# Last head's stores on GpSimd's queue, the last pair's inputs loaded before the final loop, the last convolution group kept in SBUF, and sums interleaved with splits

## The chip, the cores and the metric

The kernel runs on one core of a Trainium2 chip. The core has five engines with a queue each: TensorE (PE in the profile; PEld is its weight load), VectorE (DVE), ScalarE (ACT), GpSimd (POOL) and SyncE (SP). SyncE, ScalarE and GpSimd can start DMA transfers; the rows that end in q (SPq, ACTq) are such issues. An engine runs its queue in order, and waits at an instruction whose inputs or whose buffer aren't ready. The metric is the time of one execution on the device in microseconds (us).

## What is computed

One layer over 1024 latent tokens of width 1024, with 256 context tokens. Cut to what matters:

```python
shift, scale, gate = adaln(c, w_ada, b_ada)
h  = rmsnorm(x, norm_g) * (1 + scale) + shift
hc = rmsnorm(ctx, norm_g) * (1 + scale_c) + shift_c
q, k, v, za, u, bg, cg, zc = split(h @ w_in)       # eight groups of 512 columns
q, k = rmsnorm(heads(q), q_norm_g), rmsnorm(heads(k), k_norm_g)
kc, vc = split(hc @ w_in[:, 512:1536])              # kc is normed too
attn = neighbourhood_attention(q, k, v, kc, vc, rpb) * silu(za)    # 8 heads of 64
conv = bg * conv3(cg * u, conv_w, conv_b) * silu(zc)
out = x + gate * (concatenate([attn, conv]) @ w_out)
```

Everything is in 32-bit floats. Attention sees a clamped window of 8 by 16 tokens of the 16 by 64 grid and all context tokens in one softmax.

## The kernel before

**Tiles.** A tile has 128 partitions. Activations are held transposed: features on partitions, 1024 tokens along the row. The features of the concatenated branches are eight blocks f of 128: 0 to 3 are the four pairs of attention heads, 4 to 7 the four convolution groups. A 32-bit product is made of three matmuls: each operand is split into a high part (a cast on ScalarE) and a low part (a subtraction on VectorE), and high by high, high by low and low by high are summed in PSUM. `split` makes such a pair; `split_right` does it for activations and `split_left` for weights.

**Stages.** First the modulation and the norm, then the projection of q, k and v, then the attention of eight heads, and last the output projection. The gates and convolutions are not a stage of their own: they are cut into ticks of six matmuls, and `fill` (a generator over `attn_group` and `conv_group`) issues a tick at chosen points of the attention (`TICKS`). A `unit` is one column block of 128 outputs of w_in: two halves of 512 tokens, four ticks each, 48 matmuls, and each half has a PSUM bank of the tag "U", of which there are two. `chore` queues the ScalarE and VectorE work that follows; `do_acts` and `do_dves` issue it.

**The attention's end.** The last convolution group is `conv_group(3)`. When the attention's last quarter is issued, two ticks of its gate (the SiLU's argument) and its whole last unit (48 matmuls) are left. In `conv_group`, `gates` multiplies the convolution by the SiLU and `gains` by the last unit; `times` does either, and at the second it stores the half to `y_d` in DRAM. `head.finish` copies a head's sums and its output out of PSUM and stores them to `rs_d` and `o_d`; the queue is SyncE's, for the last head ScalarE's. The last pair of heads is then gated in pieces: `recip` loads the sums, takes reciprocals on VectorE and stores them to `ri_d`; `load_sums` loads them spread over partitions (`rb`); `z_d` holds the gate's argument, which is loaded into `zs` and goes through SiLU; and o_d, zs and rb are multiplied. The loop over the rest of `fill` at line 1432 issues one tick, then the queued chores, then `step(k)`, which holds a piece of the output projection's preparation.

**The output projection.** It is one step of a fast matrix multiplication: the 1024 by 1024 by 1024 product is cut into two by two by two blocks of 512 and made of seven products (numbered 1 to 7) instead of eight. `K_HALVES` says which feature blocks form the two halves of the inner dimension: 4, 5, 6, 0 and 1, 2, 3, 7. `combined(q)` makes the sums and differences of activation blocks, on VectorE; those of the weights lie in `w_d` from before. `load_left` loads the four raw weight blocks of a product into one of two buffers "A" and "B". `product(q, ps)` runs 48 matmuls: four inner blocks, four output tiles, three matmuls. The products run in the order 1, 5, 2, 6, 3, 7, 4. `four("SSCC")` takes the banks of the accumulator `a`, into which products 1, 6, 7 and 4 are summed in turn; `four("OOUU")` takes four others, which products 5, 2 and 3 use one after another. `residual` loads a tile of x (named m), `add` adds a bank times the gate to it (VectorE), and `put` stores it.

**What sets the order.** In the projection and the attention, instructions of TensorE, ScalarE, VectorE and GpSimd run in the order in which the program issues them (`ordered`, `strict`); from line 1340 SyncE's transfers do too. The split buffers have six ("left") and eight ("right") places in each of two pools, `op` and `rp`; a place is written again when TensorE has read it. `rp` lies where the activations of the input projection were. All instructions carry line 71 in the profile, since they are recorded by the wrapper there; the transfers of the attention carry their own lines.

Of the kernel before, what the change touches and what calls it, by code (L numbers as in the profile page):

```python
# [10 lines left out]
F32 = mybir.dt.float32  # L11
F32R = mybir.dt.float32r
BF16 = mybir.dt.bfloat16
AF = mybir.ActivationFunctionType
ALU = mybir.AluOpType
# [4 lines left out]
P = 128  # L20
D = 1024
T = 1024
# [4 lines left out]
NH, HD = 8, 64  # L27
# [28 lines left out]
def body(tc, es, x, xb, xt, cb_, ct, w_mod, w_gate, b_ada, w_grp, w_col, q_g, k_g, bias, w_out, vecs, cst, out):  # L56
# [309 lines left out]
        chore(on_act, on_dve)  # L366

    loaded = {}
    ahead = {}
    follows = {}  # L370

# [27 lines left out]
    def blocked(v):  # L399
        return v.rearrange("p (b r c) -> p b r c", b=2, r=16)  # L400

    def by_row(v):
        return v.rearrange("p (r b c) -> p b r c", r=16, b=2)
# [7 lines left out]
    def conv_group(i, done=None):  # L411
# [52 lines left out]
                taps(*work.pop(0))  # L464

        def times(half, v, last):
            dve.tensor_tensor(by_row(cvs[half][:]), blocked(v), by_row(cvs[half][:]), ALU.mult)
            if last:
                sp.dma_start(y_d[4 + i][:, half * 512:(half + 1) * 512], cvs[half])

        def gains():
# [389 lines left out]
    class head:  # L861
# [91 lines left out]
        def finish(self):  # L953

            sums = ap.tile([P, 256], F32, name="sums", tag="sums", bufs=1)
            act.copy(sums[:].rearrange("p (r c) -> p r c", c=16), self.tot[:, :256].rearrange("p (c r) -> p r c", r=16))
            queue = sp if self.h + 1 < NH else act
            queue.dma_start(rs_d[self.p][self.s].rearrange("b (x c) -> (b x) c", c=256),
                          sums[:].rearrange("(x o) c -> x o c", o=32)[:, 0])
            ob = ap.tile([P, 512], F32, name="ob", tag="ob", bufs=1)  # L960
            act.copy(blocked(ob[:]), self.po.rearrange("p (b c r) -> p b r c", b=2, r=16))
            for bank in range(2):
                queue.dma_start(o_d[self.p][64 * self.s:64 * self.s + 64, bank * 512:(bank + 1) * 512], ob[64 * bank:64 * bank + 64])  # L963
# [281 lines left out]
    vts = [prp.tile([P, NB + 2, HD], F32, name=f"v{i}", tag=f"v{i}") for i in range(2)]  # L1245
    ri_last = prp.tile([P, 64], F32, name="ri")

    left_raw, raw_y = {}, {}

    def left_rows(q, i):  # L1250

        if q in (1, 2, 4):
# [8 lines left out]
        for i in range(4):  # L1261
            sp.dma_start(left_raw[q][:, i], left_rows(q, i))

    def load_y(v, f, queue=None):
        (queue or sp).dma_start(v, y_d[f])
        raw_y[f] = v.rearrange("p (a n) -> p a n", a=2)

    def early_loads(n):
# [116 lines left out]
    def split_left(q, pl, steps=range(4)):  # L1385
        for i in steps:
            left[q, i] = split(pl, "left", 6, left_raw[q][:, i], lambda v: v)
# [27 lines left out]

    def step(k):

        if k == 2:
            for _ in reciprocals:
                pass  # L1420
        if k < 4:
            split_right(1, op, [k])
            split_left(1, op, [k])
        if k in (4, 5):
            combined(5, range(2 * k - 8, 2 * k - 6))
        if k in (5, 6):
            split_right(5, op, range(2 * k - 10, 2 * k - 8))
        if k in (7, 8):
            split_left(5, op, [k - 7])

    late = [op.tile([P, T], F32, name="y", tag="y", bufs=2)[:] for _ in range(2)]
    for k, _ in enumerate(fill):
        do_dves()
        do_acts()
        step(k)
    while soon or slow:
        do_dves()
        do_acts()
    hs.close()
    rp = es.enter_context(sbuf("rp", side="right"))  # L1440

    last = NPAIR - 1
    raw_y[last] = late[0].rearrange("p (a n) -> p a n", a=2)
    parts = []
    for half in range(2):
        cols = slice(half * 512, (half + 1) * 512)
        zs, rb = (rp.tile([P, 512], F32, name=n, tag="t", bufs=4) for n in ("zs", "rb"))
        sp.dma_start(zs, z_d[last][:, cols])
        sp.dma_start(raw_y[last][:, half], o_d[last][:, cols])
        load_sums(last, half, rb, pool)  # L1450
        parts.append((raw_y[last][:, half], zs, rb))
    load_y(late[1], 7, pool)
    load_left(2, "A")
    m12, m22 = zip(*[(residual(c, 1), residual(4 + c, 1)) for c in every_tile])
    m11 = [residual(c, 0) for c in every_tile]

    split_right(2, rp, range(2))
    split_left(5, op, [2])
    for tb, zs, rb in parts:
        act.activation(zs, zs, AF.Silu)  # L1460
        dve.tensor_tensor(tb, tb, zs, ALU.mult)
        dve.tensor_tensor(tb, tb, rb, ALU.mult)
    split_left(5, op, [3])
    load_left(6, "B")
    split_left(2, rp)
    split_right(2, rp, range(2, 4))
    combined(6)
    split_right(6, rp)

    a = four("SSCC")  # L1470
    c5 = four("OOUU")
# [1 line left out]
    for c in every_tile:  # L1473
        product(5, c5, [c], first=True)
        add(c5[c], c, m12[c])
        add(c5[c], 4 + c, m22[c])
    for c in every_tile:
        add(a[c], c, m11[c])
    load_left(3, "A")
    c2_ = four("OOUU")  # L1480
    product(2, c2_, first=True)
    split_left(6, rp)
# [1 line left out]
    split_right(3, op)  # L1484
    split_left(3, op)
    load_left(4, "A")
    combined(7)
    split_right(7, op)
    combined(4)
    for c in every_tile:  # L1490
        add(c2_[c], c, m11[c])
        put(m11[c], c, 0)
    for c in every_tile:
        product(6, a, [c])
    m21 = [residual(4 + c, 0) for c in every_tile]
# [12 lines left out]
    for c in every_tile:  # L1508
        product(7, a, [c])
        add(a[c], 4 + c, m22[c])  # L1510
        put(m22[c], 4 + c, 1)
    head_, tail = slice(0, 384), slice(384, 512)
    for c in range(3):
        product(4, a, [c])
        add(a[c], 4 + c, m21[c])
        put(m21[c], 4 + c, 0)
    end = {3: bank("pout", "O")}
    add(a[3], 7, m21[3], tail)
    product(4, a, [3], cols=head_)
    product(4, end, [3], first=True, cols=tail)  # L1520
    add(a[3], 7, m21[3], head_)
# [64 lines left out]
```

## Time and profile before

| What | Value |
| --- | --- |
| Median of 3 runs | 603.13 us (602.87 to 603.36) |
| The profiled execution | 603.09 us |
| Its span, first to last instruction | 601.3 us |
| TensorE busy | 585.5 us |
| VectorE busy | 439.8 us |
| ScalarE busy | 285.8 us |
| GpSimd busy | 56.7 us |
| Mean granted TensorE clock | 0.997 of full speed |
| Moved by DMA | 127.16 MB |

The profiled execution takes 1.8 us more than its span, for what lies ahead of the first and behind the last instruction. In a timeline row stand the start, the time taken, the engine, the operation with its tiles (out<-in, partitions by elements), how many alike are merged into the row, and in brackets the idle time before it with what ended that. In a row of merged instructions the time goes from the start of the first to the end of the last. In a row of windows stand, for each engine, the busy time and the number of instructions, then the granted clock of TensorE, the mean busy share of the 16 DMA engines and GB/s.

### The profile page before, as it was taken

Reading aid. Unit: us, or ns where it says so; the run is one execution under the profiler, and the core shown is the slowest. Engines: PE = TensorE matmul, PEld = TensorE weight load, DVE = VectorE, ACT = ScalarE, POOL = GpSimd, SP = SyncE. Lnnn points to the kernel's source line nnn. Section 1 sums busy time; section 2 is a strip of 40 time slices with the busy share of each in tenths; the row PEclk is TensorE's granted clock in tenths of the full one; section 3 lists DMA queues with packets and bytes.
Section 4 is the critical chain, followed back from the end, with each engine's and each line's share of the span. In section 5 each row is a group of like instructions: output and inputs, shape, how many; then the busy total and the mean of one; then the engine's idle time right before and its main releaser. Section 6 shows DMA issues by size and latency. Waiting matters only on the chain. (4 is left out here: it accounts for less than half of the span.)

```text
span 601.3 us, 9494 instructions
## 1 busy us (share of the span) xinstructions
PE 585.5 (97%) x3307; PEld 493.0 (82%) x3308; DVE 439.8 (73%) x898; ACT 285.8 (48%) x660; POOL 56.7 (9%) x80
## 2 busy tenths in 40 slices
PE   8999999999999999999999999999999998989997
PEld 3567899999999999888878787878878776867886
DVE  1576879756837745458989797999798896589952
ACT  6645355436526445434554473646456446345220
POOL 1001024123223232100000000000000001100000
PEclk9999999999999999999999999999999998999999
DMA  8996476945756694766162829274955631693532
GB/s 311 416 417 228 179 246 189 312 157 201 262 182 224 230 334 172 280 237 221 53 236 101 289 80 309 85 273 134 327 165 190 197 120 33 198 377 109 183 118 87
DMA packets 67148, 127.16 MB, mean 211 GB/s; under 512 B 8737, under 2 KB 27673, under 8 KB 64796
## 3 DMA queue, kind: packets, MB, share of 16 engines
q1 hardware_dynamic: 66532, 125.22, 59.8%
q0 software_dynamic: 400, 1.07, 0.5%
q8 instruction: 26, 0.43, 0.3%
q10 hardware_dynamic: 168, 0.27, 0.2%
q14 instruction: 22, 0.18, 0.1%
HBM read 92.90 MB, written 33.62 MB: 210 GB/s over the span
## 5 line engine op out<-in xcount | busy, mean ns | idle before, releaser
L71 PE MATMUL pu<-h,uh 128*128 128x512 f32 x544 | 173.3, 400 | 2.9 <-ACT zs L71 2.9
L71 PE MATMUL pacc<-w,h 128*128 128x384 f32 x768 | 138.9, 337 | 0.9 <-ACT ub L71 0.5
L71 PEld LDWEIGHTS pacc<-w,h 128*128 128x128 f32 x768 | 132.7, 188 | 1.8 <-ACT ub L71 0.9
L71 PEld LDWEIGHTS pu<-h,uh 128*128 128x128 f32 x544 | 98.1, 190 | 22.0 <-ACT zs L71 3.3
L71 PE MATMUL pu<-h,ul 128*128 128x512 f32 x272 | 107.3, 394 | 0.0
L71 PE MATMUL pout<-right,left 128*128 128x512 f32 (+2 forms) x348 | 78.6, 385 | 4.4 <-DVE m L71 3.3
L71 PEld LDWEIGHTS pout<-right,left 128*128 128x128 f32 x348 | 63.9, 188 | 19.2 <-DVE m L71 3.8
L71 PEld LDWEIGHTS pu<-h,ul 128*128 128x128 f32 x272 | 51.4, 189 | 11.6
L71 POOL TENSOR_TENSOR ss<-ss,few 128x4 f32<-128x4 f32 (+1 forms) x40 | 41.4, 1036 | 126.7 <-DVE ss L71 126.4
L71 ACT ACTIVATE sc<-sc 128x512 f32<-128x512 f32 x32 | 20.2, 633 | 37.9 <-DVE sc L71 37.9
L71 PE MATMUL acc<-h,w 128*128 128x512 f32 x144 | 37.2, 403 | 0.8 <-ACT h L71 0.8
L71 ACT ACTIVATE sq<-pacc 128x256 f32<-128x256 f32 x32 | 12.4, 387 | 46.4 <-PE pacc L71 45.7
L71 ACT COPY mg<-pmx 128x256 f32<-128x256 f32 (+1 forms) x33 | 12.1, 367 | 47.0 <-issue 22.8
L71 PEld LDWEIGHTS acc<-h,w 128*128 128x128 f32 x144 | 25.8, 188 | 9.0 <-ACT h L71 1.7
L71 DVE TENSOR_TENSOR sum<-sum,sb 128x372 f32<-128x372 f32 (+2 forms) x64 | 31.0, 485 | 2.7
L71 ACT ACTIVATE qn<-pacc,ss 128x64 f32<-128x64 f32 x128 | 30.1, 331 | 4.9 <-PE trA L71 2.5
L71 DVE TENSOR_TENSOR mx<-mx,sb 128x372 f32<-128x372 f32 (+2 forms) x64 | 30.9, 483 | 1.9
L71 DVE SCALAR_TENSOR_TENSOR m<-pout,ab,m 128x512 f32<-128x512 f32 (+2 forms) x34 | 22.5, 715 | 13.3 <-PE pout L71 13.3
L71 DVE TENSOR_REDUCE ss<-sq 128x4 f32<-128x260 f32 (+1 forms) x40 | 15.7, 392 | 21.1 <-ACT sq L71 21.1
L71 DVE TENSOR_TENSOR ul<-uraw,uh 128x512 fp32r<-128x512 f32 x34 | 23.1, 685 | 10.0 <-ACT uh L71 10.0
L71 DVE TENSOR_TENSOR sb<-pss,bt 128x192 f32<-128x192 f32 (+3 forms) x48 | 27.5, 601 | 2.8 <-PE pss L71 2.8
L71 ACT CAST left<-wraw 128x512 fp32r<-128x512 f32 x28 | 16.3, 618 | 26.9 <-PE pout L71 11.5
(142 smaller groups left out, 893.7 us busy)
## 6 DMA issues: line engine op xcount, KB each, us to landing
uraw<-in_w_col SPq DMA_DIRECT2D x34, 256.0 KB
slab<-in_w_mod SPq DMA_DIRECT2D x8, 1024.0 KB
q_d<-qs SPq DMA_DIRECT2D x32, 256.0 KB
k_s<-k_d SPq DMA_DIRECT2D x8, 1024.0 KB
q_s<-q_d SPq DMA_DIRECT2D x16, 512.0 KB
wr<-in_w_grp SPq DMA_DIRECT2D x40, 192.0 KB
bt<-in_rpb SPq DMA_DIRECT2D x8, 564.0 KB
xn<-in_xb SPq DMA_DIRECT2D x8, 512.0 KB
```

The costliest lines, as they stand in the source:

```text
L71: i = emit(*a, **kw)
```

## The change

1. `head.finish`: the last head's three stores (sums, and the output in two halves) are issued on GpSimd's queue instead of ScalarE's.
2. `conv_group`, `times`: the last group's last product is written into the tile `raw_y[7]` in SBUF instead of in place; the two stores to `y_d` and the load of `y_d[7]` go.
3. The loop over the rest of `fill`: `step` runs one tick later (k - 1). The last pair's inputs (z_d into `zs`, o_d into `raw_y[last]`) are loaded ahead of the loop, in tiles of their own in `op`; `rb`'s first half is loaded at step 1, right behind the reciprocals; the two SiLUs of `zs` and `load_left(2, "A")` come at step 4. The reciprocals move from step 2 to step 1, so they stay at the same tick.
4. Behind the loop: only `rb`'s second half is loaded; `load_left(6, "B")` goes ahead of the residuals m11; the gating of the last pair is cut into `attended(0)` and `attended(1)`, which stand at other places; the splits of product 2's weights are cut in two; `load_left(3, "A")` moves up.
5. Product 5's loop: `split_right(6)` is issued in pieces behind the sums of tiles 1, 2 and 3 instead of ahead of all products.
6. The sums of product 2 and their stores come ahead of `combined(7)`.
7. The sum of the tail of a[3] comes ahead of the loop over product 4's first three tiles.

```diff
@@ conv_group, times
-            dve.tensor_tensor(by_row(cvs[half][:]), blocked(v), by_row(cvs[half][:]), ALU.mult)
-            if last:
+            here = raw_y[7][:, half] if last and i == 3 else cvs[half][:]
+            dve.tensor_tensor(by_row(here), blocked(v), by_row(cvs[half][:]), ALU.mult)
+            if last and i < 3:
                 sp.dma_start(y_d[4 + i][:, half * 512:(half + 1) * 512], cvs[half])
@@ head.finish
-            queue = sp if self.h + 1 < NH else act
+            queue = sp if self.h + 1 < NH else pool
@@ step and the loop
-        if k == 2:
+        if k == 1:
             for _ in reciprocals:
                 pass
+            load_sums(last, 0, rb[0], pool)
         if k < 4:
             split_right(1, op, [k])
             split_left(1, op, [k])
+        if k == 4:
+            for half in range(2):
+                act.activation(zs[half], zs[half], AF.Silu)
+            load_left(2, "A")
         if k in (4, 5):
             combined(5, range(2 * k - 8, 2 * k - 6))
         if k in (5, 6):
             split_right(5, op, range(2 * k - 10, 2 * k - 8))
-        if k in (7, 8):
-            split_left(5, op, [k - 7])
-
-    late = [op.tile([P, T], F32, name="y", tag="y", bufs=2)[:] for _ in range(2)]
+        if k in (6, 7):
+            split_left(5, op, [k - 6])
+
+    last = NPAIR - 1
+    halves_of = [slice(half * 512, (half + 1) * 512) for half in range(2)]
+    for f in (last, 7):
+        raw_y[f] = op.tile([P, T], F32, name="y", tag="y", bufs=2)[:].rearrange("p (a n) -> p a n", a=2)
+    zs = [op.tile([P, 512], F32, name="zs", tag="zs", bufs=2) for _ in halves_of]
+    rb = [op.tile([P, 512], F32, name="rb", tag="rb", bufs=1)]
+    for half, cols in enumerate(halves_of):
+        sp.dma_start(zs[half], z_d[last][:, cols])
+    for half, cols in enumerate(halves_of):
+        sp.dma_start(raw_y[last][:, half], o_d[last][:, cols])
     for k, _ in enumerate(fill):
         do_dves()
         do_acts()
-        step(k)
+        if k:
+            step(k - 1)
...
-    last = NPAIR - 1
-    raw_y[last] = late[0].rearrange("p (a n) -> p a n", a=2)
-    parts = []
-    for half in range(2):
-        cols = slice(half * 512, (half + 1) * 512)
-        zs, rb = (rp.tile([P, 512], F32, name=n, tag="t", bufs=4) for n in ("zs", "rb"))
-        sp.dma_start(zs, z_d[last][:, cols])
-        sp.dma_start(raw_y[last][:, half], o_d[last][:, cols])
-        load_sums(last, half, rb, pool)
-        parts.append((raw_y[last][:, half], zs, rb))
-    load_y(late[1], 7, pool)
-    load_left(2, "A")
+    rb.append(rp.tile([P, 512], F32, name="rb", tag="t", bufs=4))
+    load_sums(last, 1, rb[1], pool)
     m12, m22 = zip(*[(residual(c, 1), residual(4 + c, 1)) for c in every_tile])
+    load_left(6, "B")
     m11 = [residual(c, 0) for c in every_tile]
 
+    def attended(half):
+
+        v = raw_y[last][:, half]
+        dve.tensor_tensor(v, v, zs[half], ALU.mult)
+        dve.tensor_tensor(v, v, rb[half], ALU.mult)
+
+    split_left(5, op, [2])
+    attended(0)
     split_right(2, rp, range(2))
-    split_left(5, op, [2])
-    for tb, zs, rb in parts:
-        act.activation(zs, zs, AF.Silu)
-        dve.tensor_tensor(tb, tb, zs, ALU.mult)
-        dve.tensor_tensor(tb, tb, rb, ALU.mult)
     split_left(5, op, [3])
-    load_left(6, "B")
-    split_left(2, rp)
+    split_left(2, rp, range(2))
     split_right(2, rp, range(2, 4))
+    split_left(2, rp, range(2, 4))
+    load_left(3, "A")
+    attended(1)
     combined(6)
-    split_right(6, rp)
@@ the products
         product(5, c5, [c], first=True)
         add(c5[c], c, m12[c])
         add(c5[c], 4 + c, m22[c])
+        if c:
+            split_right(6, rp, ((), (0, 1), (2,), (3,))[c])
     for c in every_tile:
         add(a[c], c, m11[c])
-    load_left(3, "A")
     c2_ = four("OOUU")
     product(2, c2_, first=True)
...
     load_left(4, "A")
+    for c in every_tile:
+        add(c2_[c], c, m11[c])
+        put(m11[c], c, 0)
     combined(7)
     split_right(7, op)
     combined(4)
-    for c in every_tile:
-        add(c2_[c], c, m11[c])
-        put(m11[c], c, 0)
...
     head_, tail = slice(0, 384), slice(384, 512)
+    add(a[3], 7, m21[3], tail)
     for c in range(3):
         product(4, a, [c])
         add(a[c], 4 + c, m21[c])
         put(m21[c], 4 + c, 0)
     end = {3: bank("pout", "O")}
-    add(a[3], 7, m21[3], tail)
     product(4, a, [3], cols=head_)
```

More of the change, by code (lines that the diff above doesn't have):

```diff
@@ L368, in body @@
     loaded = {}
+    left_raw, raw_y = {}, {}
     ahead = {}
@@ L1246, in body @@
     ri_last = prp.tile([P, 64], F32, name="ri")
-    left_raw, raw_y = {}, {}
     def left_rows(q, i):
@@ L1262, in load_left, with load_y @@
             sp.dma_start(left_raw[q][:, i], left_rows(q, i))
-    def load_y(v, f, queue=None):
-        (queue or sp).dma_start(v, y_d[f])
+    def load_y(v, f):
+        sp.dma_start(v, y_d[f])
         raw_y[f] = v.rearrange("p (a n) -> p a n", a=2)
```

## The prediction

> **What bounds the kernel now.** I read the busy table, then a table of windows over the last fifth, then TensorE's timeline there, and after that the timelines of ScalarE, VectorE, GpSimd and SyncE around each hole.
>
> ```profile
> PE 585.5 (97%) x3307; PEld 493.0 (82%) x3308; DVE 439.8 (73%) x898; ACT 285.8 (48%) x660; POOL 56.7 (9%) x80
> 487.00:490.00 3.00, 2.58 (x12) 2.17 (x13) 2.87 (x7) 1.71 (x3) 0.00 (x0) 1.00 0.50 173
> 499.00:502.50 3.50, 0.58 (x4) 0.16 (x2) 1.29 (x2) 3.12 (x5) 0.77 (x1) 1.00 0.35 77
> 502.50:507.50 5.00, 5.00 (x15) 3.97 (x16) 4.08 (x8) 3.48 (x7) 0.55 (x1) 0.66 0.00 0
> 526.00:538.50 12.50, 11.30 (x49) 8.71 (x47) 10.10 (x17) 6.79 (x12) 0.00 (x0) 1.00 1.04 380
> 538.50:543.50 5.00, 2.91 (x10) 1.51 (x10) 5.00 (x9) 0.20 (x1) 0.00 (x0) 1.00 0.56 211
> 487.43 0.32 PE L71 MATMUL pmx<-ci,rm 128*128 128x128 f32 x1 [0.45 <-DVE rm L71]
> 499.14 0.39 PE L71 MATMUL pu<-h,ul 128*128 128x512 f32 x1
> 502.44 0.73 PE L71 MATMUL pu<-h,uh 128*128 128x512 f32 x2 [2.92 <-ACT zs L71]
> 515.08 13.54 PE L71 MATMUL pout<-right,left 128*128 128x512 f32 x59
> 529.75 8.68 PE L71 MATMUL pout<-right,left 128*128 128x512 f32 x37 [1.13 <-DVE left L71]
> 539.59 0.94 PE L71 MATMUL pout<-right,left 128*128 128x512 f32 x3 [1.16 <-DVE m L71]
> 540.82 0.96 PE L71 MATMUL pout<-right,left 128*128 128x512 f32 x3 [0.29 <-DVE m L71]
> 542.13 0.96 PE L71 MATMUL pout<-right,left 128*128 128x512 f32 x3 [0.35 <-DVE m L71]
> 543.45 49.93 PE L71 MATMUL pout<-right,left 128*128 128x512 f32 x219 [0.36 <-DVE m L71]
> 594.48 3.64 PE L71 MATMUL pout<-right,left 128*128 128x384 f32 x24 [1.10 <-DVE m L71]
> ```
>
> In a window row the columns are each engine's busy time, the granted TensorE clock, the DMA share and GB/s. TensorE is busy for 97% of the span, so almost nothing can be won beside its holes, and all that the change touches starts after 496 us. I measure a hole from start to start, because the end of a last matmul holds its latency too. The pitch of back-to-back matmuls is (49.93 - 0.39) / 218 = 0.2272 us, from the row of 219 (0.39 is the duration of a lone one, at 499.14).
>
> Losses against that pitch: from 499.14 to 502.44 are 3.30 us for one matmul, loss **3.07**. From 502.44 to 515.08 are the 48 matmuls of the last unit, 12.64 against 10.91: loss **1.73**, which is the clock: 5.00 us at 0.66 lose 1.70. From 515.08 to 529.75 are 59 matmuls: 14.67 against 13.40, loss **1.27**. From 529.75 to 539.59 are 37: 9.84 against 8.41, loss **1.43**. Then three groups of 3 matmuls (0.68 each) take 1.23, 1.31 and 1.32: losses **0.55**, **0.63**, **0.64**. From 543.45 to 594.48 are 219: 51.03 against 49.76, loss **1.27**. The sum is 10.6 us. The change can win at most this, beside the tail of about 3 us after the last matmul, which it leaves as it is.
>
> **First hole and slow clock.** The matmul at 502.44 writes the bank of the gate's first half, which the first SiLU frees.
>
> ```profile
> 496.67 0.37 ACT L71 COPY sums<-ptot 128x256 f32<-128x256 f32 x1 [3.09 <-issue]
> 496.94 0.59 ACT L71 COPY ob<-po 128x512 f32<-128x512 f32 x1
> 497.08 1.07 ACTq L958 DMA_DIRECT2D rs_d<-sums  x1
> 497.42 0.63 ACT L71 CAST uh<-uraw 128x512 fp32r<-128x512 f32 x1
> 498.19 1.12 ACTq L963 DMA_DIRECT2D o_d<-ob  x2
> 499.35 0.62 ACT L71 CAST right<-y 128x512 fp32r<-128x512 f32 x1 [1.29 <-issue]
> 499.87 0.61 ACT L71 CAST left<-wraw 128x512 fp32r<-128x512 f32 x1
> 500.50 1.28 ACT L71 ACT_TABLE_LOAD   x1
> 501.80 1.09 ACT L71 ACTIVATE zs<-pu 128x512 f32<-128x512 f32 x2
> ```
>
> ScalarE ends the weight cast at 498.05 and computes nothing until 499.35, while it issues the last head's two output stores: 1.30 us. Then come two casts of step(0), 499.35 to 500.50: 1.15 us. Then the table load of SiLU, then the first SiLU, behind which the matmul starts at 502.44. The change sends the three stores to GpSimd and runs step(0) a tick later, behind the SiLUs. So the table load can follow the cast: 498.05 instead of 500.50, 2.45 earlier. The matmul starts at 499.99, where the pitch wanted 499.37. Of the 3.07 us, 0.62 stay: **2.45 gained**. The second SiLU needs the gate's second half, whose last matmul ends at 499.53, so it isn't held.
>
> The clock falls after the hole of 2.92 us. After holes of 0.45 (at 487.43), 1.13 (at 529.75) and 1.16 (at 539.59) the windows show 1.00. With a hole near half a microsecond I take the drop as gone: **1.70 gained**. Its bounds are 0 and 1.73. The Trainium skill, "TensorE: Matmul & The Clock Gate", Part 1, says that the gate halves the clock after at least one idle window of some 3.4 us; the hole here was shorter, so by that rule the hole alone would not explain the drop, and the loss could stay. The trace has the drop right behind its only long hole, which I follow; the other answer is a rival below.
>
> What the three stores cost on GpSimd is bounded by these rows.
>
> ```profile
> 499.43 0.77 POOL L526 DMA_DIRECT2D ri<-rs_d  x1 [106.62 <-DMA rs_d<-sums]
> 506.39 0.55 POOL L529 DMA_DIRECT2D ri_d<-ri  x1 [6.20 <-DVE ri L71]
> 508.73 1.05 POOL L533 DMA_DIRECT2D rb<-ri_d  x2 [1.78 <-DMA ri_d<-ri]
> ri<-rs_d POOLq DMA_DIRECT2D x1, 8.0 KB, 2.1
> DMA to landing us min/median/max: 2.8/5.5/8.4
> ```
>
> An issue there took 0.53 to 0.77 us with VectorE at work. Behind the stores, on GpSimd's queue, wait the load of the sums (ri), the store of their reciprocals and the loads of rb; VectorE's reciprocal waits for ri, and the whole rest of its queue stands behind that. The sums' copy ends at 497.04 and the head's copy at 497.53, so three issues of 0.77 end by 499.4 and ri is issued at about 499.5, as before; it lands 2.1 later, 501.6. VectorE comes to the reciprocal at 503.6 (below), so I count 0, with 2 us in hand; rb, issued 2.34 behind the reciprocals' store as in the rows at 506.39 and 508.73, so at some 506.2, would land by 508.5 to 515 by the row's 2.8 and 8.4. The upper bound is a GpSimd queue so slow that VectorE stands still, which is the rival on the other side. ScalarE's earlier freedom costs nothing.
>
> **Second hole.** At 529.75 TensorE waits for the low half of product 5's last weight block.
>
> ```profile
> 518.05 0.62 ACT L71 CAST left<-wraw 128x512 fp32r<-128x512 f32 x1 [3.57 <-PE pout L71]
> 528.40 0.69 DVE L71 TENSOR_TENSOR y<-y,rb 128x512 f32<-128x512 f32 x1 [3.20 <-DMA rb<-ri_d]
> 529.01 3.09 DVE L71 TENSOR_TENSOR left<-wraw,left 128x512 fp32r<-128x512 f32 x5
> 510.56 5.76 SPq L71 DMA_DIRECT2D y_d<-cv  x2
> 518.57 2.09 SPq L71 DMA_DIRECT2D wraw<-in_w_out  x4
> 520.77 11.28 SPq L71 DMA_DIRECT2D m<-in_xt  x12
> 511.65 2.49 DVE L71 TENSOR_TENSOR right<-t,right 128x512 fp32r<-128x512 f32 x4
> 538.04 7.99 DVE L71 SCALAR_TENSOR_TENSOR m<-pout,ab,m 128x512 f32<-128x512 f32 x12
> ```
>
> That block stands on VectorE behind the gating of the last pair, which waited 3.20 us for rb. SyncE's queue shows why: the conv stores held it to 516, then came the pair's inputs, wraw and twelve residual loads, and the window from 526 has a DMA share of 1.04. The change drops two stores of 256 KB and a load of 512 KB, issues the pair's inputs before the loop, rb's first half at step(1), and wraw of product 2 at step(4). The o_d loads wait for GpSimd's stores, some 501; behind them on SyncE stands only wraw, whose tile is free when the last block of product 1 is split, 507.3. Then eight residuals, into memory that the last unit's activations leave by 511 (2 MB, 6 us at the 380 GB/s of the crowded window), wraw of product 6 and four residuals: m12 and m22 are there by 517, m11 by 526. All are earlier than their readers below.
>
> VectorE's order after the change, at 0.605 us for an operation of 128x512 (three pitches of the row of 4 are 2.49 - 0.69 = 1.80) : step(0) begins behind the two SiLUs and one cast, at 501.1. Up to the first sum of product 5 come 40 such operations (8 for product 1, 2 and 2 of the conv products with the gate and the last unit, 8 combinations, 4 + 4 halves for product 5, 8 for product 2, 4 of the gating) and the reciprocal at 0.2: 24.4 us, so **525.5**. On the way: the reciprocal at 503.6, the gating's first half at 515.2, product 5's last block at 517.6 to 518.2. That block's buffer is freed by product 1's second step (the wait for PE in the row at 518.05), at 511.0 + 5.45 = 516.5, in time.
>
> TensorE: last unit 499.99 + 0.11 (the first pair takes 0.73 instead of 0.62) + 10.91 = 511.0; product 1 to 521.9. It needs the last block of product 5 at about 524, six us after it is ready: **1.27 gained**. So rb may slip by nearly six us more before it costs anything.
>
> **Third to sixth hole.** Product 2 reuses product 5's banks, and each bank takes two sums of 7.99 / 12 = 0.67. Before, these began at 538.04, when TensorE was nearly through product 5, because all of product 6's halves stood ahead. After, the halves stand between the sums. Product 5 runs 521.9 to 532.8, a tile every 2.73. Sums of tile 0: 525.5 to 526.9; tile 1 (ready at 527.6): to 528.9; two halves to 530.1; tile 2 (ready at 530.3): to 531.7; a half to 532.3; tile 3 (ready at 533.0): to 534.4. Product 2 starts at 532.8 and comes to tile 3's bank nine matmuls later, at 534.9. Nothing waits: 1.43 + 0.55 + 0.63 + 0.64 = **3.25 gained**, with 0.4 us in hand at the end and some 2 us at the start of the sums, since VectorE waits for TensorE twice between. A sum that is later than that gives back what it is late, up to the whole 3.25.
>
> From here on the order per product is that of before, some ten us earlier. The sums of product 2 come ahead of combined(7), 2.7 us on VectorE; product 7 is three products away, 33 us, and VectorE kept up there with everything in the 50 us without a hole. I count 0.
>
> **Last hole.** At 594.48 the last products wait for the sum of a[3]'s tail, which stands on VectorE behind the sum of a[2]. The change puts it ahead of the loop, where its inputs are complete after product 7: **1.27 gained**. It delays the next sum by under a pitch, hidden by a product of 2.73.
>
> **The sum.** 2.45 + 1.70 + 1.27 + 3.25 + 1.27 = 9.94 us. The profiled execution took 603.09 (span 601.3), the median of the runs is 603.13, so both give **593.2 us**.
>
> **Rivals.** (1) The slow clock stays, because it isn't the hole's length that sets it: against it stand the 1.00 after the small holes. 593.2 + 1.7 = 594.9. It is the result that the Trainium skill's rule in "TensorE: Matmul & The Clock Gate", Part 1, leaves open. (2) VectorE comes to product 5's sums over 2 us late, by waits on DMA or ScalarE that my count of 40 leaves out, and TensorE waits at the banks again: for it speaks that VectorE is the fuller engine here, with 5.00 of 5.00 from 538.5; up to 593.2 + 3.25 = 596.4. (3) The change doesn't do what it says at the attention's end: table load and SiLUs stay behind something else on ScalarE, so the first hole and its clock remain: 593.2 + 2.45 + 1.70 = 597.3. Against it: nothing else was queued there. (4) The other side, slower: GpSimd's queue, with three more issues and two waits on transfers, brings ri late, VectorE stands at the reciprocal, and all halves and sums move. The reciprocal is due at 503.6 and the sums have 2 us in hand; beyond a landing at 505.6 each microsecond costs one, and the gain of 9.9 is used up at a landing near 515.5, against 501.6 by the rows. The 106 us that GpSimd waited before were for its input. (5) The first bank comes free at the pitch: 592.6.
>
> The Trainium skill, "SBUF — State Buffer", Who interferes with whom, speaks against GpSimd's queue: its transfers starve while VectorE runs an operation in a two-port mode, for which it names copies and tensor_scalar, not tensor_tensor. It gives 3.1 us instead of 0.62 in such a case; as an estimate from that page, four issues would bring ri 9.9 us late, to 511.5, and the time to about 599. The rows above, 0.53 to 0.77 beside tensor_tensor, agree with the exception.
>
> **How the numbers follow.** Forecast 0.65 (593.2, within 0.6 for the estimates of VectorE and 0.2 of scatter), (1) 0.08, (2) 0.14, (3) 0.05, (4) 0.05, of which 0.03 slower, 0.01 level and 0.01 still faster, (5) 0.03. 0.2% is 1.2 us, about what a measurement of this kernel can tell from no change. All but (4) are faster by more: 0.95 + 0.01 = 0.96. The range from 592.4 to 596.6 takes in the forecast, (1), (2) and (5) and leaves out (3) and (4), 0.10, and the edges.
>
> **What would show it.** After, ScalarE's table load follows the cast at once, TensorE's hole before the last unit is under 0.7 us, and the clock is 1.00 from 500 to 510. The last unit takes 10.9 us; from its start to the last matmul there is no hole over 0.3 us. The reciprocal isn't waited for by more than a microsecond, and the first sum of product 5 lies some 8 us ahead of product 2's fourth bank. A hole in front of product 2, a VectorE wait on ri or rb, or a clock below 1.00 there would make the number wrong.

## The result: 592.72 us instead of 603.21, and the profile after

The changed kernel takes 592.72 us (median of 4 runs, 592.25 to 592.89), the kernel before beside it 603.21 (4 runs, 602.87 to 603.36). The ratio is 0.9826, with a 95% interval from 0.9809 to 0.9843. The prediction was 593.2 us in a range from 592.4 to 596.6. The profiled execution of the changed kernel took 592.64 us with a span of 590.8. One execution of all that follow ran at a low clock from end to end (976.99 us at a mean clock of 0.557, the kernel with the longer hole) and is left out of every comparison.

First TensorE's timeline of the changed kernel, from the gate's last matmuls to the end (start, time taken, instruction, and in brackets the wait before it).

```profile
499.00 0.39 PE L71 MATMUL pu<-h,ul 128*128 128x512 f32 x1
499.88 0.73 PE L71 MATMUL pu<-h,uh 128*128 128x512 f32 x2 [0.49 <-ACT zs L71]
...
510.89 77.00 PE L71 MATMUL pout<-right,left 128*128 128x512 f32 x348
```

All 348 matmuls of the output projection now stand in one row without a wait. Of the holes of before only the first is left, 0.49 us long; from start to start it loses 0.88 - 0.23 = 0.65 us. The last unit takes 11.01 us, against 48 pitches of 10.91. By the prediction's count of 10.6 us of losses, 0.75 remain, so 9.84 went. The spans differ by 10.5; the rest is 0.25 in the last 24 matmuls (77.00 less 324 pitches is 3.39, against 3.64 behind a hole), 0.27 after the last matmul (590.8 - 587.89, against 601.3 - 598.12) and 0.14 ahead of the first row, about the scatter of single runs.

The same kernel in windows (busy time of TensorE, its weight load, VectorE, ScalarE and GpSimd, the granted clock, DMA share, GB/s):

```profile
500.00:505.00 5.00, 5.00 (x23) 4.12 (x24) 4.15 (x8) 5.00 (x11) 0.55 (x1) 1.00 0.43 131
505.00:510.00 5.00, 5.00 (x24) 4.14 (x23) 5.00 (x10) 2.22 (x4) 2.10 (x4) 1.00 0.39 121
...
522.00:533.00 11.00, 11.00 (x50) 9.13 (x49) 9.75 (x16) 3.47 (x6) 0.00 (x0) 1.00 0.74 245
```

The clock is 1.00 where it was 0.66 before. Cut to the stretch itself, the drop before is half the clock for 3.4 us, which is the loss of 1.7:

```profile
503.70:507.10 3.40, 3.40 (x9) 2.65 (x8) 3.40 (x7) 2.28 (x5) 0.55 (x1) 0.50 0.00 0
```

The last row of the changed kernel is the stretch of product 5; its DMA share is 0.74, where before it was 1.04 (526 to 538.5): the transfers start earlier and are spread over a longer time, and in the whole kernel 126.11 MB are moved instead of 127.16.

ScalarE of the changed kernel:

```profile
497.28 0.63 ACT L71 CAST uh<-uraw 128x512 fp32r<-128x512 f32 x1
497.93 1.28 ACT L71 ACT_TABLE_LOAD   x1
499.23 1.09 ACT L71 ACTIVATE zs<-pu 128x512 f32<-128x512 f32 x2
...
504.36 1.16 ACT L71 ACTIVATE zs<-zs 128x512 f32<-128x512 f32 x2
```

The table load follows the cast at once, at 497.93 instead of 500.50, and the last pair's SiLUs run at 504.36 instead of 520. VectorE shows how far ahead it has come:

```profile
503.26 0.24 DVE L71 RECIPROCAL ri<-ri 128x16 f32<-128x16 f32 x1
...
525.61 1.40 DVE L71 SCALAR_TENSOR_TENSOR m<-pout,ab,m 128x512 f32<-128x512 f32 x2
527.41 1.41 DVE L71 SCALAR_TENSOR_TENSOR m<-pout,ab,m 128x512 f32<-128x512 f32 x2 [0.39 <-PE pout L71]
...
532.85 1.41 DVE L71 SCALAR_TENSOR_TENSOR m<-pout,ab,m 128x512 f32<-128x512 f32 x2 [0.71 <-PE pout L71]
```

The reciprocal doesn't wait for ri. The first sum of product 5 starts at 525.61 instead of 538.04, while TensorE is only 4 us earlier than before. In front of the second and the last pair of sums VectorE waits for TensorE (0.39 and 0.71 us). The last pair ends at 534.26, and product 2 wants that bank at 510.89 + 105 pitches = 534.75: 0.5 us in hand there, 1.6 with VectorE's waits. And GpSimd:

```profile
497.21 0.80 POOL L960 DMA_DIRECT2D rs_d<-sums  x1 [104.53 <-ACT sums L71]
498.00 1.09 POOL L965 DMA_DIRECT2D o_d<-ob  x2
499.31 0.57 POOL L528 DMA_DIRECT2D ri<-rs_d  x1 [0.22 <-issue]
```

Three more issues stand on its queue, 0.5 to 0.8 us each, and the load of ri is issued at 499.31, against 499.43 before.

### The profile page after: what moved, and what is told of

The parts are those of the page before. It is cut to its first block, busy times and chain, and to the rows that moved or that the text cites. A ratio compares the mean times of both kernels' runs of the same rounds, so it can differ in the third digit from the quotient of the medians.

```text
span 590.8 us, 9493 instructions
## 1 busy us (share of the span) xinstructions
PE 582.0 (99%) x3307; PEld 492.3 (83%) x3308; DVE 439.6 (74%) x898; ACT 284.8 (48%) x660; POOL 57.8 (10%) x82
## 2 busy tenths in 40 slices
DMA packets 66676, 126.11 MB, mean 213 GB/s; under 512 B 8713, under 2 KB 27649, under 8 KB 64324
## 4 chain that ended last, share of the span: by engine, by line
PE 82%; DVE 7%; DMA 5%; ACT 2%; issue 2%; SPq 1%; POOL 0%; DVEq 0%; ACTq 0%
PE pu L71 24%; PE pacc L71 22%; PE pout L71 13%; PE acc L71 5%; PE cacc L71 4%; PE po L71 4%; DMA xn<-in_xb 3%; PE pss L71 3%; PE pc L71 2%; DVE sb L71 2%; PE pmx L71 2%; PE tr L71 1%; DVE mx L71 1%; DMA rs_d<-sums 1%; PE trA L71 1%
## 5 line engine op out<-in xcount | busy, mean ns | idle before, releaser
L71 PE MATMUL pout<-right,left 128*128 128x512 f32 (+2 forms) x348 | 77.0, 383 | 0.0
L71 DVE TENSOR_TENSOR qs<-trA,qs 128x512 fp32r<-128x512 f32 x16 | 11.1, 692 | 21.2 <-ACT qs L71 18.3
```

The costliest lines, as they stand in the source:

```text
L71: i = emit(*a, **kw)
```

## The experiments

All start from the changed kernel. Times are medians, beside 592.72 of the changed kernel itself.

### The attention's end: two edits that are not two terms

The prediction gave 1.30 us to the stores and 1.15 to the order of step. Three kernels undo one, the other and both.

```diff
-            queue = sp if self.h + 1 < NH else pool
+            queue = sp if self.h + 1 < NH else act
```

> The changed kernel with the last head's three stores on ScalarE's queue again. My theory: ScalarE issues two of them between the cast and the table load, 1.30 us, so the hole before the last unit grows from 0.49 to about 1.8 us and the time from 592.7 to 594.0 with a clock of 1.00; should a hole of 1.8 already drop the clock, to about 595.7. Rival (the order of step alone made the gain, and the stores hide in ScalarE's idle time): hole 0.5, 592.7.

```diff
-        if k:
-            step(k - 1)
+        step(k)
```

> The changed kernel with step(k) at its old tick, so that the two casts of step(0) stand ahead of the SiLUs again (the other steps move up a tick too). My theory: 1.15 us more on ScalarE before the table load, hole about 1.6 us, clock 1.00, 593.8. Rival (the stores alone made the gain): hole 0.5, 592.7.

> Both edits undone: stores on ScalarE and step(k) at its old tick. My theory: hole 2.9 us as before the change, and with it the clock falls again for some 5 us: 592.7 + 2.45 + 1.70 = 596.9. Rival (the slow clock isn't due to the hole): the hole comes back, but not the clock, 595.2.

Measured: 592.79 with the stores on ScalarE, 593.67 with the old order, 596.27 with both. The holes ahead of the last unit were 0.50, 1.51 and 2.89 us; here are TensorE's rows with the stores put back and with the old order (the third is shown under the clock).

```profile
500.18 0.73 PE L71 MATMUL pu<-h,uh 128*128 128x512 f32 x2 [0.50 <-ACT zs L71]
500.78 0.73 PE L71 MATMUL pu<-h,uh 128*128 128x512 f32 x2 [1.51 <-ACT zs L71]
```

The first time is a miss: with the new order, the stores on ScalarE cost nothing. ScalarE's timeline with the stores alone put back shows why:

```profile
497.58 0.63 ACT L71 CAST uh<-uraw 128x512 fp32r<-128x512 f32 x1
498.23 1.28 ACT L71 ACT_TABLE_LOAD   x1
498.36 1.12 ACTq L965 DMA_DIRECT2D o_d<-ob  x2
499.53 1.08 ACT L71 ACTIVATE zs<-pu 128x512 f32<-128x512 f32 x2
```

The issue of the two output stores (498.36 to 499.48) runs beside the table load (498.23 to 499.51), which starts ahead of it. With both put back, the same issue stands ahead of the casts:

```profile
497.60 1.12 ACTq L965 DMA_DIRECT2D o_d<-ob  x2
498.75 0.62 ACT L71 CAST right<-y 128x512 fp32r<-128x512 f32 x1 [1.28 <-issue]
...
499.91 1.28 ACT L71 ACT_TABLE_LOAD   x1
```

Nothing is left to run beside it, so the casts wait until 498.75, and the table load comes after them. So the order is worth 1.0 us of the hole, with the stores on GpSimd. The move of the stores is worth nothing with the new order, and 1.4 us without it. The sum of both, 2.4 us, is what the prediction had (2.45); its division is not.

### The clock

In the kernel with both put back, the hole in the profiled execution is as long as before the change, but its windows show a clock of 1.00, and the time was 594.9. TensorE's row and the windows:

```profile
501.85 0.73 PE L71 MATMUL pu<-h,uh 128*128 128x512 f32 x2 [2.89 <-ACT zs L71]
```

```profile
500.00:505.00 5.00, 3.15 (x14) 2.61 (x15) 3.12 (x7) 4.99 (x9) 1.25 (x3) 1.00 0.38 109
505.00:510.00 5.00, 5.00 (x24) 4.14 (x23) 5.00 (x9) 2.67 (x5) 1.39 (x3) 1.00 0.57 168
```

The other runs of that kernel took 595.39 at a mean clock of 0.999, and 597.14 and 597.24 at 0.997. So the same program has the drop in some runs and not in others, for about 2 us. A mean clock of 0.997 is one drop of half the clock for 3.4 us, as in the trace before; 0.994 is two, as in the kernel with the round trip below. Of 25 runs of the kernel before that stood beside the experiments, five had a clock of 0.999 or more and took 602.14 to 602.53 (median 602.28); the 20 others lay at 0.997 or less with a median of 603.23. A longer hole tells more:

```diff
     for k, _ in enumerate(fill):
+        if k == 0:
+            for _ in range(8):
+                act.copy(rb[0], raw_y[4][:, 0])
         do_dves()
```

> Eight extra copies on ScalarE ahead of the SiLU's table load, so that TensorE's hole before the last unit is 4.7 us. If the length of the hole is what sets the clock (with a hole of 2.9 it fell in some runs and not in others), it falls in every run now: 592.7 + 4.2 + about 2 = 598.9, mean clock at most 0.997 in all. If it is chance, or something else in those runs, some stay at 596.9 with a clock of 0.999 or more.

Five runs took 598.71 to 600.04 (median 599.72), all at a mean clock of 0.994. The only trace of this kernel is of the execution at 0.557, in which TensorE's rows can't be compared; ScalarE's casts, table load and SiLUs take as long there as elsewhere (0.63, 1.28 and 1.09 us).

```profile
815.88 5.18 ACT L71 COPY rb<-y 128x512 f32<-128x512 f32 x8
821.08 1.28 ACT L71 ACT_TABLE_LOAD   x1
```

The copies put the table load off by 5.1 us (it starts 5.72 us after the start of the weight cast, instead of 0.65). So the hole at the full clock is an estimated 0.49 + 5.1 = 5.6 us, not the 4.7 that I had put on it, and of the 7.0 us lost about 1.9 are left for the clock. In all five runs it fell, by its mean for twice 3.4 us; where the drops lay, and why they cost no more than one does elsewhere, is not shown. So with the longer hole the drop came every time, while near 3 us the length alone doesn't decide it.

### The sum of the tail

```diff
-    add(a[3], 7, m21[3], tail)
     for c in range(3):
         product(4, a, [c])
...
     end = {3: bank("pout", "O")}
+    add(a[3], 7, m21[3], tail)
```

> The sum of a[3]'s tail behind the loop over product 4's tiles again. My theory: a hole of 1.1 us before the last 24 matmuls and nothing else, 592.7 + 1.27 = 594.0. Rival (the sum fits between the matmuls once all is earlier): 592.7.

Measured: 594.11 us, 1.4 more. TensorE's timeline of this kernel:

```profile
511.09 73.60 PE L71 MATMUL pout<-right,left 128*128 128x512 f32 x324
585.79 3.67 PE L71 MATMUL pout<-right,left 128*128 128x384 f32 x24 [1.10 <-DVE m L71]
```

The hole is back alone, and as large as the prediction's term: 1.10 us of waiting, and the 24 matmuls behind it take 3.67 instead of 3.39.

### The halves between the sums

```diff
     combined(6)
+    split_right(6, rp)
...
-        if c:
-            split_right(6, rp, ((), (0, 1), (2,), (3,))[c])
```

> The changed kernel with all four of product 6's halves ahead of product 5's sums again. My theory: the sums begin 2.4 us later (528.0), but no halves stand between them any more, so tile 3 is summed at 534.2 as with the change; no hole, 592.7. Rival (the order of the halves is what removed the holes ahead of product 2): up to 3.25 us more, 595.9.

Measured: 592.71 us, no change (592.32 to 592.96 in three runs, 594.26 in the profiled one). In the profiled execution TensorE has again one row of 348 matmuls, and VectorE does the halves first and the sums in two blocks:

```profile
529.66 4.04 DVE L71 SCALAR_TENSOR_TENSOR m<-pout,ab,m 128x512 f32<-128x512 f32 x6
534.49 4.04 DVE L71 SCALAR_TENSOR_TENSOR m<-pout,ab,m 128x512 f32<-128x512 f32 x6 [0.79 <-PE pout L71]
```

(The whole stage lies 1.6 us later in this run.) VectorE is still early enough to wait for TensorE, 0.79 us ahead of the last pair. The holes ahead of product 2 went because VectorE comes to the sums so much earlier, not because of their order.

### The last group and the last pair's inputs

```diff
-            here = raw_y[7][:, half] if last and i == 3 else cvs[half][:]
-            dve.tensor_tensor(by_row(here), blocked(v), by_row(cvs[half][:]), ALU.mult)
-            if last and i < 3:
+            dve.tensor_tensor(by_row(cvs[half][:]), blocked(v), by_row(cvs[half][:]), ALU.mult)
+            if last:
                 sp.dma_start(y_d[4 + i][:, half * 512:(half + 1) * 512], cvs[half])
...
+    pool.dma_start(raw_y[7].rearrange("p a n -> p (a n)"), y_d[7])
     rb.append(rp.tile([P, 512], F32, name="rb", tag="t", bufs=4))
```

> The last convolution group goes through DRAM again: two stores of 256 KB, and a load of 512 KB on GpSimd's queue behind them. My theory: the second store holds SyncE's queue to 514.3, the load is issued at 516.5 and lands near 522, two us after the split of product 2's last block wants it (520.1); 1.7 us of that are in hand at the sums, so a hole of up to half a microsecond and 592.7 to 593.5. Rival (the round trip was what held the kernel): 2 us or more.

Measured: 597.92 us, 5.2 more and far beyond what I expected: 596.34 and 596.45 in the runs at a clock of 0.999 or more, 599.38 and 600.06 at 0.997 and 0.994. VectorE, GpSimd and TensorE of this kernel:

```profile
526.02 0.69 DVE L71 TENSOR_TENSOR right<-y,right 128x512 fp32r<-128x512 f32 x1 [6.35 <-ACT right L71]
...
531.57 2.72 DVE L71 SCALAR_TENSOR_TENSOR m<-pout,ab,m 128x512 f32<-128x512 f32 x4
```

```profile
516.33 0.57 POOL L1456 DMA_DIRECT2D y<-y_d  x1 [9.75 <-DMA y_d<-cv]
```

```profile
510.41 21.92 PE L71 MATMUL pout<-right,left 128*128 128x512 f32 x96
533.12 0.94 PE L71 MATMUL pout<-right,left 128*128 128x512 f32 x3 [0.79 <-DVE m L71]
534.35 0.97 PE L71 MATMUL pout<-right,left 128*128 128x512 f32 x3 [0.29 <-DVE m L71]
536.87 0.96 PE L71 MATMUL pout<-right,left 128*128 128x512 f32 x3 [1.55 <-DVE m L71]
538.79 56.16 PE L71 MATMUL pout<-right,left 128*128 128x512 f32 x243 [0.95 <-DVE m L71]
```

The load was issued at 516.33, as I had it, but it took 9.0 us, until about 525.3; I had put some 5.5 on it. Twelve residuals, product 6's weights and rb's second half are issued between 514 and 528, and the DMA share is 0.84 from 517 to 520 and 1.04 from 520 to 526. That these are what slowed it fits, but was not tested by itself. VectorE stands 6.35 us behind the load (the bracket names ScalarE, whose cast waits for it in turn), reaches the sums at 531.57, and TensorE waits four times at the banks of product 2: 0.90 + 0.55 + 1.84 + 1.24 = 4.5 us against the pitch. Measured from the last unit's start (499.38 in this run, 499.88 with the change) the sums are 6.5 us late, of which 1.9 were in hand. The 4.5 us are more than the 3.25 at which the prediction capped a late VectorE. Then the clock falls in some runs, here to 0.50 for twice 3.4 us, from the last of the four waits on:

```profile
538.10:544.90 6.80, 6.11 (x14) 4.84 (x15) 5.67 (x9) 0.62 (x1) 0.00 (x0) 0.50 0.00 0
```

The next kernel has the round trip, and also the inputs' loads, the SiLUs, rb's first half and product 2's weights behind the loop:

```diff
-        if k == 4:
-            for half in range(2):
-                act.activation(zs[half], zs[half], AF.Silu)
-            load_left(2, "A")
...
+    for half, cols in enumerate(halves_of):
+        sp.dma_start(zs[half], z_d[last][:, cols])
+        sp.dma_start(raw_y[last][:, half], o_d[last][:, cols])
+    load_sums(last, 0, rb[0], pool)
     rb.append(rp.tile([P, 512], F32, name="rb", tag="t", bufs=4))
...
     split_left(5, op, [2])
+    for half in range(2):
+        act.activation(zs[half], zs[half], AF.Silu)
     attended(0)
```

> The round trip of the last group as in the run before, and the last pair's inputs, rb's first half, the SiLUs and product 2's weights at their old places behind the loop. My theory: both stores hold SyncE to 514, so the inputs come after 515 and product 2's weights near 523; product 5's last block is still split in time (no second hole), but VectorE reaches the sums near 529, 3.5 us late, of which 1.7 are in hand: a hole ahead of product 2 of about 1.8 us, 594.5. Rivals: nothing shows, 592.7; or the whole of the second to sixth hole returns, 592.7 + 1.27 + 3.25 = 597.2.

Measured: 599.26 us (598.10 to 599.96), all runs at a clock of 0.997, and so also above all that I had expected. It is 1.3 us more than the median with the round trip alone, but no more than that kernel's one run at the same clock (599.38), though everything in SyncE's queue came behind the stores:

```profile
507.66 6.94 SPq L71 DMA_DIRECT2D y_d<-cv  x2
```

```profile
518.98 0.69 DVE L71 TENSOR_TENSOR y<-y,zs 128x512 f32<-128x512 f32 x1 [3.78 <-DMA y<-o_d]
...
522.61 1.30 DVE L71 TENSOR_TENSOR right<-y,right 128x512 fp32r<-128x512 f32 x2 [2.21 <-ACT right L71]
...
532.15 2.72 DVE L71 SCALAR_TENSOR_TENSOR m<-pout,ab,m 128x512 f32<-128x512 f32 x4
```

```profile
524.56 8.69 PE L71 MATMUL pout<-right,left 128*128 128x512 f32 x37 [0.15 <-DVE left L71]
```

VectorE's sums begin at 532.15, 6.6 us late, by waits of 3.78 and 2.21 us for the inputs instead of one of 6.35 for y. The second hole is 0.15 us, not 1.13 (0.28 against the pitch, not 1.27): in this kernel only the gating's first half stands ahead of product 5's last block, not both. TensorE's losses here, this hole and the banks of product 2, sum up to 4.6 us against the 4.5 with the round trip alone. So once the group goes through DRAM, late inputs hide behind it, and it alone loses as much as both. Whether late inputs alone would lose as much was not run.

### GpSimd's queue, the rival that would have made it slower

```diff
     yield
+        for _ in range(8):
+            pool.tensor_scalar(ri, ri, 1.0, None, ALU.mult)
     dve.reciprocal(ri, ri)
```

> The changed kernel with eight small multiplications by 1.0 on GpSimd between the landing of ri and VectorE's reciprocal, about 8 us. My theory: VectorE stands at the reciprocal until some 509.8 instead of 503.3, 6.5 us late; 1.7 us are in hand at product 5's sums, the rest is lost ahead of product 2: 592.7 + 4.8 = 597.5, with no hole before product 5's end. Rival (there is far more in hand, and GpSimd's chain is off the path): 592.7.

> The changed kernel with 24 multiplications by 1.0 on GpSimd between the landing of ri and the reciprocal; eight of them took 3.42 us, so these take 10.3 and the reciprocal moves from 503.3 to about 511.9, 8.6 us late. My theory: 1.7 us of that are in hand, the other 6.9 are lost at the banks ahead of product 2: about 599.6, and up to 2 us more in runs where the clock falls in those holes. Rival (what is late on VectorE hides behind the DMA waits, and GpSimd's chain has more than 8 us in hand): 592.7.

(In the second kernel the range is 24.) Measured: 593.07 us with eight, 599.50 with 24 (598.51 and 598.65 at a clock of 0.997, 600.34 and 600.52 at 0.994). The first missed its aim: the eight took 3.42 us, not 8, so the reciprocal waited 1.50 us for it and the sums began at 527.01, 1.3 us late, within what was in hand. With 24, in the run at 600.34:

```profile
501.75 8.81 POOL L71 TENSOR_SCALAR ri<-ri 128x16 f32<-128x16 f32 x24 [1.49 <-DMA ri<-rs_d]
```

```profile
510.60 0.25 DVE L71 RECIPROCAL ri<-ri 128x16 f32<-128x16 f32 x1 [6.88 <-POOL ri L71]
...
532.62 2.72 DVE L71 SCALAR_TENSOR_TENSOR m<-pout,ab,m 128x512 f32<-128x512 f32 x4
```

```profile
525.41 9.70 PE L71 MATMUL pout<-right,left 128*128 128x512 f32 x40 [0.61 <-DVE left L71]
```

Measured from the last unit's start (500.25 in this run), the reciprocal is 7.0 us late and the sums 6.6; 5.9 us are lost in the better runs and 7.7 in those in which the clock falls more. By the prediction's account a reciprocal at 510.6 costs 5.0; against the pitch TensorE loses 4.7 in this trace. Of these, 0.75 are the second hole, which is back in the last row: product 5's last block had six us in hand, and VectorE is seven late. So the mechanism of the slower rival is real, at about its price, with the clock's loss on top. It did not come about because the issues took no longer than before the change.

Whether VectorE's copies would have slowed those issues, another kernel shows:

```diff
     for k, _ in enumerate(fill):
+        if k == 0:
+            for _ in range(12):
+                dve.tensor_copy(rb[0], raw_y[4][:, 0])
         do_dves()
```

> The changed kernel with twelve copies of 128x512 floats from SBUF to SBUF on VectorE (into a tile that is loaded later), which fill its idle time while GpSimd issues the last head's stores. If VectorE's copies keep GpSimd from its descriptors (the Trainium skill, SBUF — State Buffer, Who interferes with whom), the issues take some 3 us instead of 0.55 to 0.80, until the copies end; if not, they stay as they are. The time stays at 592.7 either way, since ri has 2 us in hand; it is the rows that tell.

GpSimd and VectorE of this kernel (one run, 592.18 us):

```profile
496.75 0.87 POOL L960 DMA_DIRECT2D rs_d<-sums  x1 [104.52 <-ACT sums L71]
497.62 1.09 POOL L965 DMA_DIRECT2D o_d<-ob  x2
498.92 0.60 POOL L528 DMA_DIRECT2D ri<-rs_d  x1 [0.21 <-issue]
```

```profile
495.71 5.55 DVE L71 COPY rb<-y 128x512 f32<-128x512 f32 x12
```

The copies cover all four issues, which take 0.87, 1.09 for two, and 0.60 us, against 0.80, 1.09 and 0.57 without them. The Trainium skill's warning in "SBUF — State Buffer", Who interferes with whom, that copies can starve GpSimd's transfers, did not show with these operands. That page makes it depend on a two-port mode of VectorE, and whether these copies ran in it no trace here shows.

### The table load in idle time

```diff
+        if n == 35:
+            act.activation(few[:, 5:6], ones, AF.Silu)
         if live(o) and o % 4 == 3:
```

> The changed kernel with a SiLU of one column on ScalarE in its 3 us of idle time ahead of the last head's copies, so that the table is loaded there. My theory: the SiLUs follow the cast at once and the first is done by 498.6, before TensorE wants the bank; the last hole (0.65 us against the pitch) goes, 592.1. Rival (the SiLU waits for something else than the table): hole stays, 592.7.

Measured: 592.02 us (5 runs, 591.50 to 592.24), ratio to the kernel before 0.9812, from 0.9798 to 0.9826. ScalarE and TensorE:

```profile
493.88 1.28 ACT L71 ACT_TABLE_LOAD   x1
...
498.22 0.61 ACT L71 ACTIVATE zs<-pu 128x512 f32<-128x512 f32 x1
```

The table is loaded in idle time, the first SiLU is done at 498.83, and TensorE has no wait from there to its last matmul (the 348 matmuls of the output projection follow the last unit at 510.51 in one piece). From the attention's last sums (ptot) to product 1 it takes 14.3 us instead of the changed kernel's 15.1, so the hole is gone. That the whole kernel is faster than the changed one isn't shown: its median is 0.7 us less, as the hole's 0.65 says, but the two intervals overlap (0.9809 to 0.9843 there), and the kernel with twelve copies, which ran beside it and still has a hole of 0.50, took 592.18.

## Why the prediction was right, point by point

- **What bounds the kernel**: right. Of the gain of 10.5 us, 9.84 lie in TensorE's holes after 499 us, where 9.94 were forecast. The other 0.7 lie in the last 24 matmuls, behind the last one and ahead of the first row, where the prediction had nothing, and are about the scatter of single runs.
- **First hole**: 0.62 us were forecast to stay, 0.65 stayed. Its two causes were priced at 1.30 and 1.15 as if they added up. They don't: the stores' issue cost time only because the casts stood behind it and the table load behind these. With the new order the move to GpSimd's queue is worth nothing.
- **The clock**: 1.70 us were in the profiled execution, as the window said. But the same hole has the drop in some runs and not in others, so the change took away a risk rather than a fixed term. The profiled run had it, as 20 of those 25 had; against the five without it the gain is 9.6 us instead of 10.5. The drop costs about 2 us where it falls in the kernel with both edits undone, about 1 us in the kernel before. That less is left there I put down to VectorE, which held TensorE up again later; that is argued, not shown.
- **Second hole**: it went, and the lead is as forecast. Product 5's last block is split at 517.66 (517.6 forecast), and TensorE wants it at 510.89 + 59 pitches = 524.3. That this lead is what removed the hole is shown by the reciprocal that came 7.0 us late: 0.75 us are back. That the earlier inputs alone made the lead is not shown: with late inputs and the round trip only 0.28 of the 1.27 return, which I put down to the gating's second half, which now stands behind that block; that is not tested by itself.
- **Third to sixth hole**: the time was right, and VectorE's arrival at the sums too (525.5 forecast, 525.61 measured, from 40 operations at 0.605 us; in the trace its row is unbroken but for 0.24 us of waiting). The reason was half wrong: the halves between the sums are worth nothing by themselves, the early arrival is all of it. Two prices were too light. A late VectorE costs more than the 3.25 us at which the prediction capped it: 4.5 where it came 6.5 late, so rival (2) could have gone beyond the range. And the last group's round trip was counted as one of several causes of a crowded queue and had no price of its own; undone by itself it costs 3.7 us at the banks ahead of product 2, and in some runs 3 more by the clock, because its 512 KB take 9 us where they are loaded.
- **Last hole**: 1.27 forecast, 1.4 measured by undoing it.
- **Sums of product 2 ahead of combined(7)**: counted as 0; TensorE has no wait there. It wasn't undone by itself.
- **The rivals**: the clock stayed at 1.00, VectorE was in time, the end of the attention did what it says, and ri was not late. The two us in hand ahead of the sums were 1.6 by the trace after, and 1.9 by the kernel with the round trip. One reading behind the price of GpSimd's issues doesn't hold: the row of 0.77 us before (from 499.43 on) stands mostly beside an idle VectorE, which had nothing to do from 498.78 to 500.00. The new issues, too, stand beside a mostly idle VectorE; the kernel with twelve copies is what shows them beside a busy one.

## What to carry to other kernels

Measure holes of a full engine from start to start against its pitch: here that made the sum 9.9 instead of the 8.5 that the bracketed waits of the last six holes would have made it, and 9.84 were found. An edit's worth depends on what else stands in the queue: two edits that clear the same wait should be priced together. Here undoing one cost nothing, undoing the other 1.0 us, and undoing both 2.4 us of waiting. And where one late input holds an in-order engine, ask how long its transfer takes among those issued with it, not how long it takes alone.

## What the runs showed of the hardware

- ScalarE's queue issued transfers beside its own table load: 1.12 us of issue, which started 0.13 us behind the load, lay within its 1.28 us at no cost, while a cast behind the same issue waited for its end. Whether the load stands ahead of the issue in the queue or is not held by it, no run shows.
- When the clock fell in a trace, it was 0.50 for 3.4 us (503.7 to 507.1 before, 540.2 to 543.6 with the round trip and late inputs) or for twice as long (538.1 to 544.9 with the round trip, 538.3 to 545.1 with the reciprocal late).
- A hole of 2.9 us in front of TensorE lowered the clock in two of four runs of one kernel, a hole of an estimated 5.6 us in all five. Four waits of 0.3 to 1.6 us within 6.5 us did it too, in some runs. The Trainium skill, "TensorE: Matmul & The Clock Gate", Part 1, has the clock fall after at least one idle window of some 3.4 us, which runs free of the kernel. The drops here are as long as that window, but holes shorter than it lowered the clock in some runs, which that rule doesn't explain; the runs decide.
- A multiplication of 128x16 floats by a constant took GpSimd 0.43 us in a series of eight and 0.37 in one of 24, not the microsecond that I had put on it from the 1.04 us of a power of 128x4 in the profile of the kernel before.
- A copy of 128x512 floats from SBUF to SBUF took VectorE 0.46 us, a subtraction of the same size 0.605.
